# Row sums of x from a token-major copy, the layer embedding normalised in the gate, and matmuls planned with a margin

## Chip, cores and metric

One core of one Trainium2 chip. The time is device microseconds of one launch.

## What is computed

One layer of a hybrid encoder on x (2048 tokens x 1024, float32), with p (2048 x 256) as a per-layer embedding:

```
hn = RMSNorm(h) ; [u|q|k|v] = hn @ W_in
y  = concat[pool_mixer(u), per-head RMSNorm(stick_breaking_attention(q,k,v))]
h  = h + RMSNorm(y @ W_out)
h  = h + RMSNorm(sqrelu(RMSNorm(h) @ W_up) @ W_down)
h  = h + sigmoid(h @ W_gate) * RMSNorm(p @ W_ple)
```

The pooling mixer takes trailing means over 2, 4, 8 and 16 positions; the attention is strictly causal with 8 heads of 64. Every RMSNorm has a gain per channel.

## The kernel before

Tokens are cut into four chunks of 512; everything stands channel-major, a tile being 128 channels x 512 tokens, a page two of them. Each product of two float32 operands is made of three matmuls on float32r halves: every operand is split by ScalarE (the rounded half, `hi`) and VectorE (the rest, `lo`); `mm3` and `proj` issue the triples. Names in the trace: `pl` the bank of p @ W_ple, `e` its tiles, `dn` a bank of a projection, `dw` a bank of W_down, `nm` a bank of a norm, `z`, `tp`, `op` banks of attention, `act` a normalised and split input, `xp` a page of x, `qk` split q, k and pooled tiles, `wh`/`wl` split weights, `acc` the W_down sums.

A norm's factor per token is a sum over channels, that is over partitions. `add_square` squares tile after tile (ScalarE) and adds the squares into `nrm` (VectorE, or POOL where it is passed); `norm` sums the columns of `nrm` with four one-column matmuls against ones (`nm<-ones,nrm`), `rstd` turns the 128 x 4 sums into factors (`ms` on VectorE, a power on POOL, `rs` on VectorE), and `spread` brings them back to all partitions: a transpose (`nm<-ident,rs`), a masked copy on VectorE (`rt`) and a matmul (`nm<-rt,sel`). `row_rstd` copies that to a page.

`prenorm` loads x of a chunk in four pages, squares and adds its eight tiles, and multiplies each by its gain and the factor (`xp<-xp,gains,nrm`) before the split. `ple` makes the embedding of a chunk: eight `pl` banks, evicted to `e`, squared, added by POOL, then normalised by VectorE (`e<-e,gains,nrm`) and stored to HBM in four pages. `gate` loads those pages much later; per tile it takes the sigmoid (ScalarE), multiplies by the embedding and adds to h (VectorE), and stores the result. `build` starts with `ple` of all four chunks, `prenorm` of chunks 0 and 1 between them, then the input projections; attention of one chunk runs among the projections and the feed-forward of others.

The order of the instructions is not that of the code. Every operation is recorded by class `Plan` with a priority, which is the TensorE work recorded before it (the constants at the top, T_PRE, T_PLE, T_ATT, R_ATT and so on, place the parts against each other). `deadlines` carries due times back from the consumers; `order` then runs a model of the engines with a price table (`cost`), hand-over times (`LATENCY`), 53 pages, 28 small tiles and 8 PSUM banks, and on each engine takes the ready operation that is due first. What it picks becomes the fixed order of each engine's instructions; on the chip each engine then waits by semaphores only. An operation's readiness in the model is one line:

```
o.ready = max(o.ready, pick.end + LATENCY[e][o.engine])
```

A bank or page that comes free is counted apart from that. All transfers are issued from SP's queue, in order.

Of the kernel before, what the change touches and what calls it, by code (L numbers as in the profile page):

```python
# [21 lines left out]
P = 128  # L22
S = 2048
D = 1024
# [17 lines left out]
PAGES = 53  # L42
BANKS = ("pl", "dn", "nm", "z", "tp", "op", "dw")
SMALL = ("ms", "rs", "halo")
T_PRE = (11.649, 22.588)
T_PLE = (0.0, 24.403, 53.992, 45.124)
T_IN = 52.377
T_ATT = 148.286
R_ATT = 4.515
R_MAIN = 1.159  # L50
T_END = 0.0
G_IN = 4
G_GATE = 3
G_OUT = 11
NORM_LAG = (34.149, 9.928)


class Buf:
# [78 lines left out]
class Engine:  # L137
# [8 lines left out]

CROSS = {"pe": 0.2, "act": 0.15, "dve": 0.155, "pool": 0.16, "sp": 0.1}
BUSY = {"pe": 0.0, "act": 2.1, "dve": 3.9, "pool": 3.4, "sp": 1.1}
LATENCY = {
    "pe": {"pe": 0.003, "act": 0.2, "dve": 0.2, "pool": 0.2, "sp": 0.1},  # L150
    "act": {"pe": 0.27, "act": 0.142, "dve": 0.13, "pool": 0.17, "sp": 0.1},
# [4 lines left out]


SLACK = 8.348
EVICT = -0.454
AHEAD = {'pe': 40.856, 'act': 24.695, 'dve': 39.763, 'pool': 35.657, 'sp': 42.237}  # L160
LEAD = {'pe': 3.156, 'act': 0.736, 'dve': 0.004, 'pool': 1.033, 'sp': 1.169}
TAIL = 40.0
WINDOW = 4096 / 1200.0

# [28 lines left out]
class Plan:  # L193
# [165 lines left out]
    def order(self):  # L359
# [42 lines left out]
        while len(result) < len(ops):  # L402
            if not events:
                raise RuntimeError(f"order: stuck after {len(result)} of {len(ops)}")
            now = heapq.heappop(events)
            while events and events[0] <= now:
                heapq.heappop(events)
            while frees and frees[0][0] <= now:
                used[heapq.heappop(frees)[2].kind] -= 1
            moved = True  # L410
            while moved:
                moved = False
                for e in CROSS:
                    p = pending[e]
                    while p and p[0][0] <= now:
                        _, prio, seq = heapq.heappop(p)
                        heapq.heappush(waiting[e], (prio, seq))
                    if free[e] > now or not waiting[e]:
                        continue
                    skipped = []  # L420
                    pick = None
                    limit = line[front].prio + AHEAD[e]
                    while waiting[e] and waiting[e][0][0] <= limit:
                        item = heapq.heappop(waiting[e])
                        if can(ops[item[1]]):
                            pick = ops[item[1]]
                            break
                        skipped.append(item)
                    for item in skipped:
                        heapq.heappush(waiting[e], item)  # L430
                    if pick is None:
                        continue
                    moved = True
                    for b in pick.allocs:
                        b.placed = True
                        used[b.kind] += 1
                        if b.first > front:
                            live[b.kind][front:b.first] += 1
                    if e == "sp":
                        free[e] = now + pick.dur[0] + 0.03  # L440
                        dma = max(dma, now + pick.dur[0] + 0.65) + pick.dur[1]
                        pick.end = dma + 0.85
                    elif e == "pe":
                        pick.end = free[e] = clock.run(now, pick.dur)
                    else:
                        pick.end = free[e] = now + pick.dur
                    heapq.heappush(events, free[e])
                    result.append(pick)
                    gone[pick.place] = True
                    while gone[front]:  # L450
                        front += 1
                    front = min(front, len(ops) - 1)
                    for b in pick.bufs:
                        b.users -= 1
                        b.end = max(b.end, pick.end + CROSS[e])
                        if not b.users and b.real is None:
                            heapq.heappush(frees, (b.end, id(b), b))
                            heapq.heappush(events, b.end)
                    for o in after[pick.seq]:
                        o.left -= 1  # L460
                        o.ready = max(o.ready, pick.end + LATENCY[e][o.engine])
                        if not o.left:
                            heapq.heappush(pending[o.engine], (o.ready, o.prio, o.seq))
                            heapq.heappush(events, o.ready)
# [15 lines left out]
class Net:  # L480
# [152 lines left out]
            self.sp.dma_start(out=t, in_=dram[:, 2 * k2:2 * k2 + 2, :])  # L633
        return t

    def prenorm(self, dram, which):
        ts = [self.load2(dram, k2, "xp") for k2 in range(4)]
        nrm = None
        for k in range(NK):
            nrm = self.add_square(nrm, ts[k // 2][:, k % 2, :])  # L640
        r = self.row_rstd(nrm)
        acts = []
        for k in range(NK):
            t = ts[k // 2][:, k % 2, :]
            self.dve.scalar_tensor_tensor(out=t, in0=t, scalar=self.g(which, k), in1=r, op0=ALU.mult, op1=ALU.mult)
            acts.append(self.pair("act", t))
        return acts
# [230 lines left out]
    def ple(self, c, p_in, dd):  # L878
        t = self.page("pin")
        with self.plan.early(12.0):  # L880
            self.sp.dma_start(out=t, in_=p_in[c])
        acts = [self.pair("pp", t[:, k, :]) for k in range(2)]
        es = []
        nrm = None
        for ot in range(NK):
            ps = self.bank("pl")
            cs = slice(ot * P, (ot + 1) * P)
            self.mm3(ps, [(self.ple_w[k][0][:, cs], self.ple_w[k][1][:, cs], acts[k][:, 0, :], acts[k][:, 1, :])
                          for k in range(2)])
            if ot % 2 == 0:  # L890
                es.append(self.page("e"))
            m = es[-1][:, ot % 2, :]
            self.act.copy(m, ps)
            nrm = self.add_square(nrm, m, self.pool)
        r = self.row_rstd(nrm)
        for k in range(NK):
            m = es[k // 2][:, k % 2, :]
            self.dve.scalar_tensor_tensor(out=m, in0=m, scalar=self.g(G_PLE, k), in1=r, op0=ALU.mult, op1=ALU.mult)
            if k % 2:
                self.sp.dma_start(out=dd["e"][c][:, k - 1:k + 1, :], in_=es[k // 2])  # L900


    def mlp_ups(self, gi, acts, w_up, dd, first, tag):
# [49 lines left out]
        return acts  # L953

    def gate(self, cs, acts, w_gate, dd, out, first):
        for ot in range(NK):
            j = ot % 2
            if j == 0:
                ge, gh, gs = [[self.page(t) for _ in cs] for t in ("geh", "geh", "gs")]
                for i, c in enumerate(cs):  # L960
                    self.sp.dma_start(out=ge[i], in_=dd["e"][c][:, ot:ot + 2, :])
                    self.sp.dma_start(out=gh[i], in_=dd["h2"][c][:, ot:ot + 2, :])
            unit = self.weight(w_gate[ot], dd["w_gate"][ot], first)
            for i, c in enumerate(cs):
                ps = self.bank("dn")
                self.proj(ps, unit, acts[i])
                s, h = gs[i][:, j, :], gh[i][:, j, :]
                self.act.activation(s, ps, AF.Sigmoid)
                self.dve.tensor_tensor(out=s, in0=s, in1=ge[i][:, j, :], op=ALU.mult)
                self.dve.tensor_tensor(out=h, in0=h, in1=s, op=ALU.add)  # L970
                if c == NCH - 1:
                    self.sp.dma_start(out=out[c][:, ot, :], in_=h)
                elif j:
                    self.sp.dma_start(out=out[c][:, ot - 1:ot + 1, :], in_=gh[i])


def build(tc, x, p, gains, w_in, w_v, w_pool, w_out, w_up, w_down, w_gate, w_ple, out):
    with (
        tc.tile_pool(name="dram", bufs=1, space=DRAM) as dp,
        tc.tile_pool(name="const", bufs=1) as cp,  # L980
# [8 lines left out]
        def dram(name, shape):  # L989
            return plan.fixed(dp.tile(shape, F32, name="d_" + name), shape)  # L990

        dd = {n: [] for n in ("q", "k", "v", "y", "h1", "h2", "e")}
        for c in range(NCH):
            dd["q"].append([dram(f"q{c}{j}", [2, HD, 2, CH]) for j in range(NPAIR)])
            dd["k"].append([dram(f"k{c}{j}", [2, 2, HD, CH]) for j in range(NPAIR)])
# [1 line left out]
            dd["y"].append([dram(f"y{c}{k}", [P, 2, CH]) for k in range(NK)])  # L997
            for n in ("h1", "h2", "e"):
                dd[n].append(dram(f"{n}{c}", [P, NK, CH]))
        for n, m in (("w_in", 12), ("w_v", 4), ("w_out", NK), ("w_up", NF), ("w_down", NF), ("w_gate", NK)):  # L1000
            dd[n] = [[dram(f"{n}{i}{a}", [P, D]) for a in range(2)] for i in range(m)]

# [3 lines left out]
        acts = {}  # L1006
        for c in range(2):
            plan.at(T_PRE[c])
            acts[c] = net.prenorm(x[c], G_PRE)
            plan.at(T_PLE[c + 1])  # L1010
            net.ple(c + 1, p, dd)
        plan.at(T_PLE[3])
# [1 line left out]

        def project(c):
            if c > 1:
                acts[c] = net.prenorm(x[c], G_PRE)
            net.in_proj(c, w_in, w_v, acts[c], dd)
            net.u_proj(c, w_in, acts[c], dd)

# [104 lines left out]
```

## Time and profile before

| | us |
|---|---|
| median of 3 runs (2662.93 to 2663.47) | 2663.43 |
| the profiled execution, its own time | 2662.55 |
| its span, first to last instruction | 2660.8 |
| TensorE busy (share) | 2626.7 (99%) |
| weight loads busy | 2146.5 (81%) |
| VectorE, ScalarE, POOL busy | 1709.8 (64%), 1037.3 (39%), 726.6 (27%) |

668 MB pass the DMA engines. Every operation stands under one line, L275, the helper that issues a recorded call, so the rows are told apart by tile names. Weight loads overlap matmuls. A TensorE that is busy 99% can still be slow, since a matmul counts as busy while it goes through; the granted clock has to be read beside it.

### The profile page before, as it was taken

The page shows a single profiled execution, that of the slowest core. Times are in us where ns is not written, and L with a number is a line of the kernel's source. Part 1 is how long each engine was busy: PE and PEld are TensorE (multiplying, and loading weights), DVE is VectorE, ACT ScalarE, POOL GpSimd, SP SyncE. Part 2 cuts the span into 40 slices and gives each one's busy share as a digit, 9 for nine tenths or more (in the row PEclk, how much of TensorE's full clock was granted, in tenths as well). Part 3 has the DMA queues.
Part 4 walks back from the last instruction along what each step waited for, and adds up shares of the span by engine and source line. Part 5 has one row for each costly group of instructions (what it writes and reads, how often), then busy time and mean ns, then how long its engine had stood idle before and what let it go on. Part 6 is the DMA issues. An engine that isn't in the chain of part 4 may idle for free.

```text
span 2660.8 us, 34134 instructions
## 1 busy us (share of the span) xinstructions
PE 2626.7 (99%) x12312; PEld 2146.5 (81%) x12312; DVE 1709.8 (64%) x2331; ACT 1037.3 (39%) x1907; POOL 726.6 (27%) x663
## 2 busy tenths in 40 slices
PE   8999999999999999999999999999999999999999
PEld 6778787777888888888888888888887888888887
DVE  7854748868777759967665568685667273433454
ACT  8433536446445445445333343443334122111111
POOL 5432335344233323323333223333334000000000
PEclk9899999999999999999999999999999999999999
DMA  6899878878777758747955476475754675555576
GB/s 260 318 370 348 287 261 327 277 242 331 258 258 257 293 190 335 280 157 279 355 192 190 159 260 252 163 257 201 281 202 158 258 270 196 207 193 196 201 287 239
DMA packets 213129, 668.41 MB, mean 251 GB/s; under 512 B 22880, under 2 KB 39264, under 8 KB 212960
## 3 DMA queue, kind: packets, MB, share of 16 engines
q1 hardware_dynamic: 212960, 666.22, 69.8%
q8 instruction: 98, 1.61, 0.2%
q14 instruction: 71, 0.58, 0.1%
HBM read 489.97 MB, written 176.16 MB: 250 GB/s over the span
## 4 chain that ended last, share of the span: by engine, by line
PE 91%; DVE 4%; DMA 1%; ACT 1%; issue 1%; POOL 1%; SPq 0%; ACTq 0%; DVEq 0%; POOLq 0%
PE dn L275 50%; PE dw L275 26%; PE op L275 4%; PE z L275 4%; PE tp L275 4%; PE nm L275 2%; DVE q L275 1%; POOL nrm L275 1%; ACT nrm L275 1%; DMA wl<-d_w_up 0%; DMA d_y<-ypool 0%; DVE nrm L275 0%; DVE e L275 0%; DVE at L275 0%; POOL pt L275 0%
## 5 line engine op out<-in xcount | busy, mean ns | idle before, releaser
L275 PE MATMUL dn<-act,wh 128*128 128x512 f32 x2816 | 901.4, 401 | 4.3 <-ACT act L275 2.2
L275 POOL TENSOR_TENSOR pr<-pr,q 128x1 f32<-128x1 f32 (+4 forms) x512 | 564.5, 1115 | 1116.0 <-ACT pr L275 481.6
L275 PE MATMUL dw<-m,wh 128*128 128x512 f32 x2048 | 644.7, 396 | 3.0 <-DVE acc L275 3.0
L275 PEld LDWEIGHTS dn<-act,wh 128*128 128x128 f32 x2816 | 510.8, 190 | 103.0 <-issue 5.3
L275 PE MATMUL dn<-act,wl 128*128 128x512 f32 x1408 | 553.0, 393 | 0.0
L275 DVE TENSOR_TENSOR_SCAN q<-q,ones 128x512 f32<-128x512 f32 (+1 forms) x320 | 401.7, 1268 | 95.2 <-ACT q L275 94.0
L275 PEld LDWEIGHTS dw<-m,wh 128*128 128x128 f32 x2048 | 374.1, 188 | 76.3 <-DVE acc L275 3.4
L275 DVE TENSOR_TENSOR acc<-acc,dw 128x512 f32<-128x512 f32 x480 | 324.8, 681 | 139.1 <-PE dw L275 137.5
L275 PE MATMUL dw<-m,wl 128*128 128x512 f32 x1024 | 400.0, 391 | 0.0
L275 PEld LDWEIGHTS dn<-act,wl 128*128 128x128 f32 x1408 | 265.9, 189 | 57.8
L275 ACT CAST at<-tp 128x512 fp32r<-128x512 f32 (+1 forms) x320 | 166.5, 524 | 302.5 <-PE tp L275 271.9
L275 DVE TENSOR_TENSOR at<-tp,at 128x512 fp32r<-128x512 f32 (+1 forms) x320 | 191.1, 602 | 125.6 <-ACT at L275 125.2
L275 DVE TENSOR_TENSOR rl<-rl 128x512 f32<-128x512 f32 x128 | 97.7, 764 | 263.7 <-ACT rl L275 263.4
L275 ACT ACTIVATE q<-z 128x512 f32<-128x512 f32 (+1 forms) x320 | 171.3, 537 | 239.0 <-PE z L275 227.7
L275 ACT ACTIVATE rl<-dn 128x512 f32<-128x512 f32 x128 | 76.6, 598 | 472.3 <-PE dn L275 462.6
L275 PEld LDWEIGHTS dw<-m,wl 128*128 128x128 f32 x1024 | 192.2, 188 | 41.5
L275 POOL TENSOR_TENSOR ms<-ms,mhalf 128x4 f32<-128x4 f32 (+1 forms) x36 | 55.2, 1534 | 614.8 <-DVE ms L275 614.7
L275 PE MATMUL op<-at,kv 128*128 128x512 f32 (+3 forms) x640 | 182.9, 365 | 2.0 <-DVE at L275 2.0
L275 PE MATMUL z<-kv,qd 128*128 128x512 f32 (+3 forms) x640 | 178.1, 361 | 0.0
L275 ACT ACTIVATE pr<-z 128x512 f32<-128x512 f32 (+1 forms) x320 | 170.2, 534 | 5.2 <-PE op L275 2.6
L275 PE MATMUL tp<-ident,pr 128*128 128x128 f32 x1088 | 169.7, 272 | 1.2 <-DVE acc L275 0.6
L275 PEld LDWEIGHTS tp<-ident,pr 128*128 128x128 f32 x1088 | 136.0, 140 | 39.8 <-DVE acc L275 1.1
(118 smaller groups left out, 2961.7 us busy)
## 6 DMA issues: line engine op xcount, KB each, us to landing
wh<-d_w_up SPq DMA_DIRECT2D x96, 512.0 KB, 4.9
wl<-d_w_up SPq DMA_DIRECT2D x96, 512.0 KB, 6.0
wh<-d_w_down SPq DMA_DIRECT2D x96, 512.0 KB, 5.5
wl<-d_w_down SPq DMA_DIRECT2D x96, 512.0 KB, 5.2
xin<-d_h SPq DMA_DIRECT2D x48, 512.0 KB, 7.2
kv<-d_k SPq DMA_DIRECT2D x80, 256.0 KB, 6.1
kv<-d_v SPq DMA_DIRECT2D x80, 256.0 KB, 6.6
wh<-d_w_in SPq DMA_DIRECT2D x36, 512.0 KB, 8.1
```

The lines of the kernel that those rows point to most:

```text
L275: fn(*[a.real() if isinstance(a, Ref) else a for a in args], **{k: a.real() if isinstance(a, Ref) else a for k, a in kw.items()})
```

## The change

It does three things, and sets new values for the planner's constants.

1. x is passed a second time, token-major (`xr`, 128 tokens x 1024). `prenorm` loads four such tiles per chunk, and ScalarE squares each with a running sum over its row, which gives the sums per token directly: no squares of x tiles, no adds, no matmuls against ones. `rstd` and `spread` follow as before.
2. `ple` stores `e` unnormalised, page by page as it is evicted, and adds the squares on VectorE; the factor row goes to HBM as a tile of its own (`er`). `gate` loads that row, multiplies by embedding and gain in one instruction, by the row in a second, and adds.
3. In the planner an operation of TensorE is ready 2 us later than its input from another engine.

```diff
+MARGIN = 2.0
...
-T_ATT = 148.286
-R_ATT = 4.515
+T_ATT = 158.048
+R_ATT = 4.132
...
-                        o.ready = max(o.ready, pick.end + LATENCY[e][o.engine])
+                        late = MARGIN if o.engine == "pe" and e != "pe" else 0.0
+                        o.ready = max(o.ready, pick.end + LATENCY[e][o.engine] + late)
...
+    def token_sums(self, rows):
+        sums = self.plan.tile([P, 16], F32, "ms")
+        for b in range(4):
+            t = self.plan.tile([P, D], F32, "xr")
+            with self.plan.early(8.0):
+                self.sp.dma_start(out=t, in_=rows[b])
+            self.act.activation(t, t, AF.Square, accum_out=sums[:, b:b + 1])
+        return sums[:, 0:4]
-    def prenorm(self, dram, which):
+    def prenorm(self, dram, rows, which):
+        rs = self.rstd(self.token_sums(rows), 4, D)
         ts = [self.load2(dram, k2, "xp") for k2 in range(4)]
-        nrm = None
-        for k in range(NK):
-            nrm = self.add_square(nrm, ts[k // 2][:, k % 2, :])
-        r = self.row_rstd(nrm)
+        with self.plan.resumed(self.plan.t + NORM_LAG[1]):
+            bank = self.spread(rs, self.bank("nm"))
+        r = self.page("nrm")[:, 1, :]
+        self.act.copy(r, bank)
...
-            nrm = self.add_square(nrm, m, self.pool)
-        r = self.row_rstd(nrm)
-        for k in range(NK):
-            m = es[k // 2][:, k % 2, :]
-            self.dve.scalar_tensor_tensor(out=m, in0=m, scalar=self.g(G_PLE, k), in1=r, op0=ALU.mult, op1=ALU.mult)
-            if k % 2:
-                self.sp.dma_start(out=dd["e"][c][:, k - 1:k + 1, :], in_=es[k // 2])
+            nrm = self.add_square(nrm, m)
+            if ot % 2:
+                self.sp.dma_start(out=dd["e"][c][:, ot - 1:ot + 1, :], in_=es[-1])
+        self.sp.dma_start(out=dd["er"][c], in_=self.row_rstd(nrm))
...
+        rows = []
+        for c in cs:
+            rows.append(self.page("er")[:, 0, :])
+            self.sp.dma_start(out=rows[-1], in_=dd["er"][c])
...
-                self.dve.tensor_tensor(out=s, in0=s, in1=ge[i][:, j, :], op=ALU.mult)
+                self.dve.scalar_tensor_tensor(out=s, in0=s, scalar=self.g(G_PLE, ot), in1=ge[i][:, j, :], op0=ALU.mult,
+                                              op1=ALU.mult)
+                self.dve.tensor_tensor(out=s, in0=s, in1=rows[i], op=ALU.mult)
                 self.dve.tensor_tensor(out=h, in0=h, in1=s, op=ALU.add)
```

The new constants (T_PRE, T_PLE, G_IN, NORM_LAG, EVICT, AHEAD, LEAD beside the two above) and the margin change the order on every engine. Three places:

VectorE while chunk 0 is projected, around a norm's masked copy `rt`. Before:

```order
47 L275 TENSOR_TENSOR wl<-ws,wh 128x1024
48 L275 SCALAR_TENSOR_TENSOR e<-e,gains,nrm 128x512
49 L275 CAST rs<-ms 128x4
50 L275 SCALAR_TENSOR_TENSOR e<-e,gains,nrm 128x512
51 L275 TENSOR_TENSOR qk<-dn,qk 128x512
52 L275 TENSOR_TENSOR rs<-ms,rs 128x4
53 L275 SCALAR_TENSOR_TENSOR e<-e,gains,nrm 128x512 x6
54 L275 TENSOR_TENSOR rt<-nm,pick_84 8x512
55 L275 TENSOR_TENSOR qk<-dn,qk 128x512
56 L275 TENSOR_TENSOR wl<-ws,wh 128x1024 x3
```

With the change:

```order
64 L276 TENSOR_TENSOR nrm<-nrm 128x512 x3
65 L276 TENSOR_TENSOR qk<-dn,qk 128x512
66 L276 TENSOR_SCALAR ms<-nm 128x4
67 L276 TENSOR_TENSOR nrm<-nrm 128x512
68 L276 CAST rs<-ms 128x4
69 L276 TENSOR_TENSOR wl<-ws,wh 128x1024
70 L276 TENSOR_TENSOR rs<-ms,rs 128x4
71 L276 TENSOR_TENSOR nrm<-nrm 128x512
72 L276 TENSOR_TENSOR qk<-dn,qk 128x512
73 L276 TENSOR_TENSOR rt<-nm,pick_84 8x512
74 L276 TENSOR_TENSOR nrm<-nrm 128x512
75 L276 TENSOR_TENSOR wl<-ws,wh 128x1024
```

The normalisations of `e` are gone, and the adds of squares (`nrm`) stand in ones and twos between the splits.

TensorE at the start, the embedding's matmuls and the first two norms. Before:

```order
3 L275 MATMUL pl<-pp,plew 128x512 x6
4 L275 MATMUL nm<-ones_76,nrm 128x1 x4
5 L275 MATMUL pl<-pp,plew 128x512 x9
6 L275 MATMUL nm<-ident,rs 8x128
7 L275 MATMUL pl<-pp,plew 128x512 x6
8 L275 MATMUL nm<-rt,sel_92 128x512
9 L275 MATMUL pl<-pp,plew 128x512 x6
10 L275 MATMUL nm<-ident,rs 8x128
```

With the change:

```order
1 L276 MATMUL pl<-pp,plew 128x512 x48
2 L276 MATMUL nm<-ident,rs 8x128
3 L276 MATMUL pl<-pp,plew 128x512 x15
4 L276 MATMUL nm<-rt,sel_92 128x512
5 L276 MATMUL pl<-pp,plew 128x512 x27
6 L276 MATMUL nm<-ident,rs 8x128
7 L276 MATMUL pl<-pp,plew 128x512 x18
8 L276 MATMUL nm<-rt,sel_92 128x512
9 L276 MATMUL pl<-pp,plew 128x512 x15
```

The column sums ahead of the first transpose are gone, the transpose comes after 48 matmuls, and 15 and 18 matmuls stand between it and the spread.

SP's queue at the start. Before:

```order
2 L275 DMA pin<-in_p 128x1024
3 L275 DMA ws<-in_w_ple 128x512 x4
4 L275 DMA xp<-in_x 128x1024 x2
5 L275 DMA pin<-in_p 128x1024
6 L275 DMA xp<-in_x 128x1024 x3
7 L275 DMA pin<-in_p 128x1024
8 L275 DMA xp<-in_x 128x1024 x2
9 L275 DMA ws<-in_w_in 128x1024
10 L275 DMA pin<-in_p 128x1024
11 L275 DMA xp<-in_x 128x1024
12 L275 DMA ws<-in_w_in 128x1024 x5
13 L275 DMA ws<-in_w_v 128x1024 x2
```

With the change:

```order
2 L276 DMA pin<-in_p 128x1024
3 L276 DMA ws<-in_w_ple 128x512 x4
4 L276 DMA xr<-in_xr 128x1024 x4
5 L276 DMA pin<-in_p 128x1024
6 L276 DMA xr<-in_xr 128x1024 x4
7 L276 DMA pin<-in_p 128x1024
8 L276 DMA ws<-in_w_in 128x1024
9 L276 DMA xp<-in_x 128x1024 x2
10 L276 DMA pin<-in_p 128x1024
11 L276 DMA xp<-in_x 128x1024
12 L276 DMA d_e_156<-e 128x1024
13 L276 DMA xp<-in_x 128x1024
```

Eight row copies go ahead of x and of the first weights, and stores of `e` stand among the loads.

## Rows read from the trace of the kernel before

**Rows 1.** The page: span, engines' busy us, one group (count, busy us, mean ns).
```profile
span 2660.8 us, 34134 instructions
...
PE 2626.7 (99%) x12312; PEld 2146.5 (81%) x12312; DVE 1709.8 (64%) x2331; ACT 1037.3 (39%) x1907; POOL 726.6 (27%) x663
...
L275 DVE TENSOR_TENSOR rl<-rl 128x512 f32<-128x512 f32 x128 | 97.7, 764 | 263.7 <-ACT rl L275 263.4
```

**Rows 2.** TensorE's waits, who ended them: us in total, times, longest.
```profile
PE pl L275 <- ACT plew L275: 6.9, 1, 6.9
PE nm L275 <- DVE rt L275: 5.9, 2, 3.6
PE dw L275 <- DVE acc L275: 3.0, 1, 3.0
PE nm L275 <- DVE rs L275: 2.2, 2, 2.0
PE dn L275 <- DVE at L275: 2.2, 1, 2.2
PE dn L275 <- ACT act L275: 2.2, 1, 2.2
PE dn L275 <- DVE act L275: 2.1, 3, 1.7
PE op L275 <- DVE at L275: 2.0, 6, 0.5
...
PE dn L275 <- DVE qk L275: 0.3, 1, 0.3
```

**Rows 3.** The chain of waits at the end: start, us, what.
```profile
2592.91 62.80 PE dn L275 x276
...
2657.09 0.69 DVE geh L275
```

**Rows 4.** By stretch: PE, PEld, DVE, ACT, POOL us; PEclk, DMA share, GB/s.
```profile
40.00:70.00 30.00, 29.61 (x132) 23.32 (x131) 28.73 (x34) 22.92 (x41) 21.24 (x11) 1.00 0.49 181
70.00:104.00 34.00, 28.11 (x98) 21.81 (x98) 28.79 (x36) 16.03 (x27) 20.53 (x13) 0.80 0.81 301
104.00:270.00 166.00, 165.65 (x786) 134.37 (x785) 93.29 (x143) 64.55 (x124) 41.12 (x38) 1.00 1.02 357
270.00:300.00 30.00, 26.04 (x123) 20.17 (x122) 27.97 (x45) 20.10 (x44) 15.98 (x13) 0.89 0.57 193
...
400.00:460.00 60.00, 56.97 (x271) 46.41 (x270) 54.72 (x61) 42.13 (x78) 37.35 (x28) 0.97 0.87 317
```

**Rows 5.** The timeline of VectorE, 55 to 78 us: start, us, what.
```profile
64.50 10.30 DVE L275 SCALAR_TENSOR_TENSOR e<-e,gains,nrm 128x512 f32<-128x512 f32 x6
74.73 0.67 DVE L275 TENSOR_TENSOR rt<-nm,pick 8x512 fp32r<-8x512 f32 x1
```

**Rows 6.** Groups of VectorE's instructions, 2050 to 2661 us.
```profile
L275 DVE TENSOR_TENSOR rl<-rl 128x512 f32<-128x512 f32 x42 | 29.0, 692 | 161.5 <-ACT rl L275 161.5
...
L275 DVE SCALAR_TENSOR_TENSOR acc<-acc,gains,nrm 128x512 f32<-128x512 f32 x16 | 11.0, 749 | 2.1 <-ACT nrm L275 2.1
```

**Rows 7.** Groups of all engines' instructions, 0 to 100 us.
```profile
L275 POOL TENSOR_TENSOR nrm<-nrm 128x512 f32<-128x512 f32 x28 | 51.9, 1870 | 37.2 <-ACT nrm L275 37.2
...
L275 DVE SCALAR_TENSOR_TENSOR e<-e,gains,nrm 128x512 f32<-128x512 f32 x9 | 14.7, 1675 | 0.6 <-ACT nrm L275 0.6
...
L275 DVE TENSOR_TENSOR nrm<-nrm 128x512 f32<-128x512 f32 x14 | 12.5, 893 | 9.2 <-ACT nrm L275 9.1
```

**Rows 8.** Groups of TensorE's instructions by shape, whole span.
```profile
L275 PE MATMUL nm<-ones,nrm 128*128 128x1 f32 x160 | 19.9, 245 | 0.6 <-POOL nrm L275 0.5
```

**Rows 9.** The chain of waits at the start: start, us, what.
```profile
3.60 6.42 DMA xp<-in_x
```

**Rows 10.** Two more stretches, columns as in rows 4.
```profile
10.00:20.00 10.00, 10.00 (x45) 8.22 (x44) 4.99 (x6) 8.72 (x17) 2.60 (x2) 1.00 1.03 415
2200.00:2400.00 200.00, 200.00 (x886) 165.19 (x886) 80.05 (x122) 32.25 (x53) 1.40 (x1) 1.00 0.54 194
```

More of the change, by code (lines that the diff above doesn't have):

```diff
@@ L44 @@
 SMALL = ("ms", "rs", "halo")
-T_PRE = (11.649, 22.588)
-T_PLE = (0.0, 24.403, 53.992, 45.124)
+T_PRE = (12.427, 26.975)
+T_PLE = (0.0, 23.664, 53.992, 38.428)
 T_IN = 52.377
-T_ATT = 148.286
-R_ATT = 4.515
+T_ATT = 158.048
+R_ATT = 4.132
 R_MAIN = 1.159
 T_END = 0.0
-G_IN = 4
+G_IN = 6
 G_GATE = 3
 G_OUT = 11
-NORM_LAG = (34.149, 9.928)
+NORM_LAG = (33.412, 9.928)
 class Buf:
@@ L158 @@
 SLACK = 8.348
-EVICT = -0.454
-AHEAD = {'pe': 40.856, 'act': 24.695, 'dve': 39.763, 'pool': 35.657, 'sp': 42.237}
-LEAD = {'pe': 3.156, 'act': 0.736, 'dve': 0.004, 'pool': 1.033, 'sp': 1.169}
+EVICT = -0.605
+AHEAD = {'pe': 42.752, 'act': 24.695, 'dve': 39.763, 'pool': 24.241, 'sp': 42.237}
+LEAD = {'pe': 3.156, 'act': 0.736, 'dve': 0.004, 'pool': 1.033, 'sp': 1.078}
 TAIL = 40.0
@@ L974, in gate, with build @@
                     self.sp.dma_start(out=out[c][:, ot - 1:ot + 1, :], in_=gh[i])
-def build(tc, x, p, gains, w_in, w_v, w_pool, w_out, w_up, w_down, w_gate, w_ple, out):
+def build(tc, x, xr, p, gains, w_in, w_v, w_pool, w_out, w_up, w_down, w_gate, w_ple, out):
     with (
@@ L990, in dram @@
             return plan.fixed(dp.tile(shape, F32, name="d_" + name), shape)
-        dd = {n: [] for n in ("q", "k", "v", "y", "h1", "h2", "e")}
+        dd = {n: [] for n in ("q", "k", "v", "y", "h1", "h2", "e", "er")}
         for c in range(NCH):
@@ L999, in build @@
                 dd[n].append(dram(f"{n}{c}", [P, NK, CH]))
+            dd["er"].append(dram(f"er{c}", [P, CH]))
         for n, m in (("w_in", 12), ("w_v", 4), ("w_out", NK), ("w_up", NF), ("w_down", NF), ("w_gate", NK)):
@@ L1008, in build @@
             plan.at(T_PRE[c])
-            acts[c] = net.prenorm(x[c], G_PRE)
+            acts[c] = net.prenorm(x[c], xr[c], G_PRE)
             plan.at(T_PLE[c + 1])
@@ L1016, in project @@
             if c > 1:
-                acts[c] = net.prenorm(x[c], G_PRE)
+                acts[c] = net.prenorm(x[c], xr[c], G_PRE)
             net.in_proj(c, w_in, w_v, acts[c], dd)
@@ L1102 @@
         "x": _chunks(np.asarray(x)[0]),
+        "xr": np.asarray(x)[0].reshape(NCH, CH, D)[:, ::-1].reshape(NCH, 4, P, D),
         "p": _chunks(np.asarray(p)[0, 0]),
```

## The prediction

> **What bounds the kernel now.** I read the page's engine shares first: TensorE is busy 2626.7 of 2660.8 us [rows 1], so only what holds TensorE up matters. The list of TensorE's waits came next [rows 2]: the first row is the start, and the other eleven sum to 21.6 us. The rest of the idle time is the end, 5.1 us from the last matmul at 2655.71 [rows 3] to the span's end. Then the table by stretch, for the granted clock [rows 4]. Where its mean is under 1.00, TensorE ran part of the stretch at the lower of its two levels, 1.2 instead of 2.4 GHz, and the time lost is length times (1 - clock): 34 x 0.20 = 6.8 us in 70 to 104, 30 x 0.11 = 3.3 us in 270 to 300, 60 x 0.03 = 1.8 us in 400 to 460, together 11.9 us. Before each of these TensorE waited, so it goes when the wait goes. Waits and clock, 33.5 us, are what an order that never lets TensorE wait could win.
>
> By name the waits are of four kinds [rows 2]. **`rt`**: 5.9 us in two pieces, both in 70 to 104. VectorE shows why [rows 5]: the small `rt` stood behind six `e` normalisations, 10.30 us in a row, 1.7 us each. Alone such an instruction takes 0.75 us (the `acc` row [rows 6], same operation and shape); beside them POOL was adding squares, 28 adds of 1870 ns, with VectorE's own adds at 893 [rows 7]. **`act`**: 2.2 + 2.1 us, where the first matmuls of chunk 2 come before their operand; the low clock in 270 to 300 goes with it. **Inputs that come a little late**: `rs` 2.2, `at` 2.2 and 2.0, and three small ones, 7.8 us, spread over the span. **`acc`**: 3.0 us and a small one, 3.6, an add that has to free a PSUM bank. (Three rows under 0.7 us are left out ahead of the last; with it they are 2.0.)
>
> **The change, part by part.**
>
> *Early VectorE queue.* The 32 `e` normalisations leave this stretch, as do 14 adds of prenorm's squares (9 and 14 fall within the first 100 us: 14.7 + 12.5 = 27.2 us [rows 7]); the 28 adds of POOL come to VectorE, 28 x 0.69 (a product of that shape in a POOL-free stretch [rows 6]) = 19.3 us. POOL is left with the `ms` powers, so the slowing beside it should go as well. The order bears it out: ahead of the `rt` now stand single adds and `qk` or `wl` splits, no row of six. I take 11.7 of the 5.9 + 6.8 = 12.7 us; ends 0 and 12.7. Next late there would be a `wl` split.
>
> *Chunk 2.* Its chain loses seven adds of squares and a set of column sums, but the order shows TensorE as short of work as before: between chunk 2's `nm<-rt` and its first `dn<-act` stand 4.2 us of matmuls instead of 1.4 us, while that chain needs a copy, four normalisations at 0.75, a cast and a subtraction, and two `o` steps stand between: eight or nine steps of about 0.7 us, some 6 us. A wait of 2 us remains, with some low clock. I take 3 of 4.3 + 3.3 = 7.6 us; ends 0 and 7.6.
>
> *The margin.* The planner now calls a matmul ready 2 us later than its input from another engine. The first spread of a norm, for one, has 15 matmuls between its two halves where it had 6. Counted over both whole orders at 0.227 us per 512 columns (62.80 us for 276 of them [rows 3]), waits of TensorE with under 2.5 us of matmuls between the last matmul they depend on and themselves were 43 and are 20; 14 stand in the chunk-2 hole in either order, so elsewhere 29 become 6. From the third kind, with its clock, 7.8 + 1.8 = 9.6 us, I take 7.5; ends 0 and 9.6. The margin acts on inputs, not on a bank coming free, so of the 3.6 us for `acc` I take 1.5.
>
> *Small terms.* Sixteen column-sum matmuls of prenorm go: 19.9 / 160 = 0.124 us each [rows 8], 2.0 us. The end grows: behind the last sigmoid stood a product and a sum, 0.7 us each [rows 3]; now one instruction of 0.75 and two of 0.69, +0.75 us. ScalarE changes 32 squares for 16 twice as long, which is no more work. The eight er transfers (256 KB each) and the gate's extra multiplies are covered: VectorE is busy 64% [rows 1].
>
> *The start.* The eight row copies of chunks 0 and 1 come ahead of x on SP, and four squares ahead of the first `e<-pl` on ScalarE. The first x copy lands at 3.60 + 6.42 = 10.0 us [rows 9]; a row copy takes its place, and three more follow at 0.52 MB / 415 GB/s = 1.26 us [rows 10], the last at 13.8. One square more, about 1.1 us, and the first eviction starts near 15 us. Eight PSUM banks of six matmuls last from 6.9 to 17.8 us: covered. The second p tile is two transfers later (2.5 us), which may show: +1 us; ends 0 and +4.
>
> *New waits.* A wholly new order has new misses; I put +4, ends 0 and 21.6 (as many as now).
>
> A rule that speaks against the gate's part: the Trainium skill (SBUF — State Buffer, "Who interferes with whom") says that a VectorE instruction with two SBUF inputs and a GpSimd instruction that reads SBUF lock each other out for a whole instruction. By it each of the 16 added multiplies of the first two gates could stand behind a whole POOL instruction, and nothing would be won at `acc`. What the rows show there is milder: the `rl` product takes 764 ns over the whole span [rows 1], 692 where POOL is idle [rows 6]. By the rule the result would be 2645 or 2646.
>
> **Sum.** -11.7 - 3 - 7.5 - 1.5 - 2.0 + 0.75 + 1 + 4 = -20 us against the profiled execution's own 2662.55 (span 2660.8 and 1.75 around it): 2642.6. The median shown, 2663.43, lies 0.9 higher, so 2643.5. With every term at its good end: -12.7 - 7.6 - 9.6 - 3.6 - 2.0 + 0.75 = -34.8, 2629.
>
> The Trainium skill (Perfetto Trace Analysis, "Identifying the Most-Contended Engine") holds matmul busy time for a bad measure and weight-load busy for a good one. Taken against the gapless stretch 2200 to 2400, where weight loads fill 165.2 / 200 = 82.6% [rows 10], the 2146.5 us of them [rows 1] would need 2599 us: 62 us of room instead of 33.5. No wait is named for the other 28, so they are not in the range.
>
> **Rivals.** *The waits only move.* The planner's prices are not the chip's (an `e` step of 0.75 us took 1.7), so a new order can miss as often as the old. Then the new waits are 21.6 and not 4, and the result is 2643.5 + 17.6 = 2661. That the margin does nothing on the chip ends here too. The count of 43 to 20 speaks against it. Chance 0.11.
>
> *The transfers become the bound.* Until 270 us the kernel moves 12 row copies of 0.52 MB and four er rows, 7.3 MB more. Between 104 and 270 the DMA engines are at 1.02 of their time and move 357 GB/s [rows 4]: there 7.3 MB cost 20.5 us. Between 40 and 104 us there is idle DMA time of 30 x 0.51 + 34 x 0.19 = 22 us, so it just fits, and only if SP's in-order queue fills it. SP stood there because its stores wait for their data, and the order now puts `e` stores, which wait for ScalarE, between the weight loads. If hardly any of it is filled, weights come late by 20.5 us, and the clock falls behind the waits; at the cheapest ratio seen (1.8 us of clock for the 2.2 us wait and two small ones, 3.0, in 400 to 460) that is 33 us: 2676. It decides once some 15 of the 20.5 us are not absorbed. Against it: TensorE has no wait on a transfer today but the start, and the store of each `e` tile no longer waits for its norm. Chance 0.12, slower.
>
> **How the numbers follow.** The forecast has 0.72, the rivals 0.11 and 0.12, the rest lies between. The forecast's own range is 2629 to 2656. To leave out no more than 2 in 10 I go up to 2664: the first rival in, most of the second out. 0.2% is 5.3 us, about what a measurement of this kernel can tell from no change. Faster: the forecast, part of the first rival and of the rest, 0.75; within: 0.11; slower: 0.14.
>
> **What would show it.** Early queue: no wait of TensorE on `rt` over 1 us before 110 us and clock 1.00 between 40 and 104; `e` gone from VectorE's products there, its `nrm` adds near 0.69 us. Margin: TensorE's waits past 300 us under 6 us in sum, clock 1.00 in 400 to 460. Chunk 2: a wait for `act` near 270 us remains. End: three VectorE instructions behind the last sigmoid. Wrong: waits on landings of `wl` or `xp` between 30 and 270 us, or as many waits on VectorE as now in new places.

## The result

The changed kernel takes **2639.29 us** (median of 4 runs, 2638.64 to 2640.74) where the kernel before, timed beside it, takes 2663.18 (2660.91 to 2663.47): a ratio of 0.9913, 95% interval 0.9896 to 0.993. That is 23.9 us less, against the 20 forecast, and 4.2 us under the predicted 2643.5. The profiled execution took 2640.74 us, 21.8 less than the 2662.55 of the one before. Its page:

```profile
span 2638.9 us, 34111 instructions
...
PE 2612.6 (99%) x12280; PEld 2135.4 (81%) x12280; DVE 1702.4 (65%) x2331; ACT 1030.8 (39%) x1907; POOL 680.8 (26%) x635
```

The busy times of VectorE and POOL fell by 7 and 46 us [rows 1], neither of which sets the end. TensorE's waits, which answer to [rows 2] (us in total, times, longest):

```profile
PE pl L276 <- ACT plew L276: 7.2, 1, 7.2
PE op L276 <- DVE at L276: 6.2, 4, 1.8
PE nm L276 <- DVE rt L276: 1.8, 2, 0.9
PE op L276 <- issue: 1.4, 1, 1.4
PE dn L276 <- DVE act L276: 0.9, 2, 0.7
PE dw L276 <- DVE at L276: 0.9, 1, 0.9
PE tp L276 <- DVE acc L276: 0.7, 1, 0.7
PE dn L276 <- ACT act L276: 0.6, 1, 0.6
PE nm L276 <- DVE rs L276: 0.4, 1, 0.4
PE dn L276 <- DVE qk L276: 0.3, 1, 0.3
```

Here `plew` is the split W_ple and `pp` the split p, `pr` a page of attention weights, `at` its transposed and split copy, `o` the attention output. Besides the start the waits are 13.2 us, 21.6 before. `rt` went from 5.9 to 1.8, `acc` (3.0) is gone, but `op<-at` grew from 2.0 to 6.2. The stretches, in the columns of [rows 4] (PE, PEld, DVE, ACT, POOL busy us with counts; granted clock, DMA share, GB/s), first of the changed kernel:

```profile
0.00:40.00 40.00, 31.93 (x132) 24.72 (x132) 22.36 (x47) 34.01 (x64) 4.46 (x45) 1.00 0.95 371
40.00:70.00 30.00, 30.00 (x135) 24.34 (x135) 26.27 (x39) 27.66 (x50) 1.99 (x1) 1.00 1.03 418
70.00:104.00 34.00, 34.00 (x156) 27.24 (x155) 15.09 (x22) 13.17 (x18) 3.55 (x5) 1.00 0.98 364
104.00:270.00 166.00, 163.97 (x793) 133.59 (x791) 89.38 (x140) 69.70 (x147) 52.89 (x48) 1.00 1.02 351
270.00:300.00 30.00, 27.53 (x136) 21.35 (x137) 29.64 (x46) 16.02 (x35) 14.85 (x10) 1.00 0.73 249
300.00:400.00 100.00, 98.44 (x481) 79.25 (x480) 60.65 (x79) 42.31 (x85) 38.29 (x34) 1.00 0.81 281
400.00:460.00 60.00, 59.95 (x294) 48.55 (x293) 42.69 (x57) 38.62 (x75) 24.45 (x20) 1.00 1.03 404
460.00:590.00 130.00, 128.19 (x619) 103.05 (x618) 102.99 (x143) 64.37 (x128) 61.31 (x47) 0.99 0.73 250
590.00:1800.00 1210.00, 1205.56 (x5800) 986.86 (x5800) 906.86 (x1160) 553.08 (x1014) 418.18 (x376) 1.00 0.69 246
1800.00:2060.00 260.00, 260.00 (x1213) 214.13 (x1212) 141.62 (x194) 69.26 (x128) 56.10 (x48) 1.00 0.63 233
2060.00:2661.00 601.00, 573.06 (x2538) 472.37 (x2536) 264.84 (x412) 102.58 (x171) 4.78 (x4) 1.00 0.59 217
```

The same cuts of the kernel before, as far as [rows 4] don't show them:

```profile
0.00:40.00 40.00, 32.39 (x141) 25.81 (x142) 23.93 (x40) 32.63 (x60) 17.60 (x55) 1.00 0.85 323
...
300.00:400.00 100.00, 99.77 (x492) 80.59 (x491) 52.97 (x82) 34.96 (x73) 30.05 (x29) 1.00 0.84 294
...
460.00:590.00 130.00, 129.93 (x630) 105.20 (x630) 91.44 (x135) 60.06 (x118) 41.40 (x36) 1.00 0.78 266
590.00:1800.00 1210.00, 1206.89 (x5787) 988.01 (x5786) 879.38 (x1146) 544.63 (x993) 403.59 (x357) 1.00 0.69 248
1800.00:2060.00 260.00, 255.69 (x1229) 210.00 (x1228) 164.66 (x203) 94.63 (x179) 91.31 (x81) 1.00 0.59 212
2060.00:2661.00 601.00, 595.70 (x2640) 490.82 (x2638) 263.95 (x412) 104.66 (x176) 6.43 (x5) 1.00 0.62 228
```

From these, idle time plus length times (1 - clock), before and after, gives a ledger of TensorE's lost time:

| stretch | before | after | difference |
|---|---|---|---|
| 0 to 104 us | 13.9 + 6.8 clock | 8.1 | -12.6 |
| 104 to 300 | 4.3 + 3.3 clock | 4.5 | -3.1 |
| 300 to 1800 | 6.4 + 1.8 clock | 7.9 + 1.3 clock | +1.0 |
| 1800 to 2060 | 4.3 | 0 | -4.3 |
| 2060 to the span's end | 5.1 | 5.8 | +0.7 |

That is -18.3 of the span's -21.9 us. The other 3.6 go with work that is gone: TensorE has 32 matmuls fewer (12312 and 12280), all of them column sums (x160 in [rows 8], now x128):

```profile
L276 PE MATMUL nm<-ones,nrm 128*128 128x1 f32 x128 | 15.1, 239 | 0.0
```

### The profile page after: what moved, and what is told of

Same layout as the page of the kernel before. It is cut to its first block, busy times and chain, and to the rows that moved or that the text cites. A ratio compares the mean times of both kernels' runs of the same rounds, so it can differ in the third digit from the quotient of the medians.

```text
span 2638.9 us, 34111 instructions
## 1 busy us (share of the span) xinstructions
PE 2612.6 (99%) x12280; PEld 2135.4 (81%) x12280; DVE 1702.4 (65%) x2331; ACT 1030.8 (39%) x1907; POOL 680.8 (26%) x635
## 4 chain that ended last, share of the span: by engine, by line
PE 92%; DVE 5%; DMA 1%; ACT 1%; issue 1%; POOL 0%; SPq 0%; DVEq 0%; ACTq 0%
PE dn L276 50%; PE dw L276 26%; PE z L276 5%; PE op L276 4%; PE tp L276 4%; PE nm L276 2%; DVE q L276 1%; PE pl L276 1%; DMA wl<-d_w_in 1%; DVE at L276 0%; DVE wl L276 0%; DVE ypool L276 0%; DMA xr<-in_xr 0%; DVE act L276 0%; DVE qk L276 0%
## 5 line engine op out<-in xcount | busy, mean ns | idle before, releaser
L276 DVE TENSOR_TENSOR_SCAN q<-q,ones 128x512 f32<-128x512 f32 (+1 forms) x320 | 409.3, 1293 | 87.0 <-ACT q L276 85.4
```

Of the source, the lines that this page charges most:

```text
L276: fn(*[a.real() if isinstance(a, Ref) else a for a in args], **{k: a.real() if isinstance(a, Ref) else a for k, a in kw.items()})
```

## The experiments

The theory was that the terms are separate and add up: 13 us of the start by taking the normalisations and POOL's adds out of one another's way, 7 or so by the margin, the rest small. The main rival was the prediction's own first one, that the waits only move with each new order. Every kernel is one edit of the kernel before or of the changed one; its time is told with its ratio to the kernel before, timed beside it, and the 95% interval of that ratio.

**1. The changed kernel without the margin.**

```diff
-MARGIN = 2.0
+MARGIN = 0.0
```

> The changed kernel with the margin set to 0, all else as in it. Theory (early VectorE queue worth about 12 us, margin about 8): no wait on rt over 1 us before 110 us and clock 1.00 there, but small waits on rs, rt and at come back after 110 us; 2645 to 2650 us. Rival (the margin does it all): the early waits come back too, 2655 to 2663.

Measured: 2654.46 us, ratio 0.9969 (0.9958 to 0.998). Up to 104 us it is as good as with the margin, and the waits stand later:

```profile
PE op L276 <- DVE at L276: 8.5, 6, 2.1
...
PE tp L276 <- POOL pr L276: 5.5, 5, 3.1
```

The `pr` waits are new; 4.9 us of them stand at 1054 to 1060 us, and in 1060 to 1080 the granted clock is 0.88. So the early gain doesn't need the margin. In this program the margin is worth 15 us, which lies between the two expectations: the theory gave it 8, the rival the whole gain.

**2. The kernel before with the margin alone.** The edit is the change's two lines in the planner.

```diff
+MARGIN = 2.0
-                        o.ready = max(o.ready, pick.end + LATENCY[e][o.engine])
+                        late = MARGIN if o.engine == "pe" and e != "pe" else 0.0
+                        o.ready = max(o.ready, pick.end + LATENCY[e][o.engine] + late)
```

> The kernel before with the 2 us margin alone. Theory: the waits past 300 us shrink by 5 to 8 us, but the wait on rt behind the e normalisations at 70 to 104 us and its low clock stay; 2652 to 2658 us. Rival (the margin does it all): 2640 to 2645.

Measured: 2664.99 us, ratio 1.0003 (0.9993 to 1.0013): no difference, and both expectations missed. The rows of 70 to 104 and of 270 to 300 us:

```profile
70.00:104.00 34.00, 29.36 (x110) 22.95 (x110) 29.16 (x36) 17.07 (x29) 15.12 (x11) 0.85 0.86 323
...
270.00:300.00 30.00, 25.50 (x115) 19.17 (x114) 28.81 (x44) 18.65 (x42) 19.11 (x15) 0.73 0.67 226
```

The early fall of the clock stays (0.85), and 270 to 300 got worse: 0.73, 8.1 us, where it was 0.89 [rows 4]. A margin that is worth 15 us in one program is worth nothing in the other.

**3. The kernel before, every engine's order as it was, POOL's adds cut short.** POOL still does the 28 adds of squares, at the same places, but on one of 512 columns; so the row sums of the layer embedding are left out.

```diff
-            nrm = self.add_square(nrm, m, self.pool)
+            nrm = self.add_square(nrm, m, self.pool, 1)
```

> The kernel before, every instruction in the same order, but POOL's 28 adds of the embedding's squares work on 1 of 512 columns (left out: the sum of the squares of the embedding in the other 511 columns). Theory (POOL and VectorE hold each other up, so that rt comes late): the six e steps take 0.75 us each instead of 1.7, the waits on rt in 70 to 104 go, with the clock there; 2649 to 2653 us, waits past 110 us as before. Rival (the queue order alone makes rt late): e steps stay at 1.7 us or the wait stays over 2 us; 2660 to 2664.

Measured: 2649.85 us, ratio 0.9952 (0.9937 to 0.9967), 13 us less with no instruction moved. VectorE's timeline at the place of [rows 5]:

```profile
58.41 4.06 DVE L281 SCALAR_TENSOR_TENSOR e<-e,gains,nrm 128x512 f32<-128x512 f32 x6
65.93 0.68 DVE L281 TENSOR_TENSOR rt<-nm,pick 8x512 fp32r<-8x512 f32 x1 [3.46 <-PE nm L281]
```

The six `e` steps take 4.06 us in place of 10.30, and now it is `rt` that waits, for TensorE. POOL's own queue is shorter too, a second way for `rt` to come earlier, but a small one: from the start of the `ms` step ahead of this row to the row's end VectorE took 18.9 us before and 7.7 here, and of that it stood idle for a result of POOL for 0.9 and 0.2 us. The rest is longer steps. In 70 to 104 us TensorE is busy throughout at full clock:

```profile
70.00:104.00 34.00, 34.00 (x156) 27.38 (x155) 28.14 (x44) 20.61 (x32) 6.46 (x12) 1.00 0.98 361
```

Its later waits are those of before (`acc` 3.0, `rs` 2.2, `at` 2.2, `act` 2.2). This is the cleanest of the runs: the early term is shown, with its cause (POOL's adds) and its size, and the row of six `e` steps is still there.

**4. The changed kernel with the planner constants of before** (`T_PRE` to `LEAD` as in the diff's minus lines; margin and code of the change kept).

```diff
-G_IN = 6
+G_IN = 4
...
-EVICT = -0.605
+EVICT = -0.454
...
```

> The changed kernel with the planner's constants (start times, rates, AHEAD, LEAD, EVICT, NORM_LAG, G_IN) of the kernel before, margin kept. Theory (the constants are fine tuning): 2639 to 2647 us. Rival (the constants carry the gain): over 2652.

Measured: 2650.32 us, ratio 0.9953 (0.9938 to 0.9968), between the two. The late wait on a bank is back, and with it the place of 400 to 460 us:

```profile
400.00:460.00 60.00, 57.33 (x267) 46.99 (x268) 40.83 (x52) 36.14 (x70) 23.76 (x22) 0.94 0.97 356
...
1800.00:2060.00 260.00, 257.00 (x1232) 211.86 (x1231) 176.40 (x222) 93.52 (x177) 93.42 (x82) 0.99 0.60 212
```

TensorE's wait in the second stretch is the one of the kernel before [rows 2]:

```profile
PE dw L276 <- DVE acc L276: 3.0, 1, 3.0
```

Every kernel run here with the new constants is busy for 260.00 of the 260 us of 1800 to 2060, with or without the margin and the code parts; every one with the old constants waits there. So the `acc` term, 3 to 4 us, belongs to the constants; which of them does it was not tried. In all the constants are worth 11 us in the changed program (2650.32 against 2639.29), nearly half of its gain, and the prediction gave them no price.

**5. The changed kernel with the old row sums of x.**

```diff
-        rs = self.rstd(self.token_sums(rows), 4, D)
...
+        nrm = None
+        for k in range(NK):
+            nrm = self.add_square(nrm, ts[k // 2][:, k % 2, :])
+        r = self.row_rstd(nrm)
```

> The changed kernel with x's row sums taken as before, by VectorE adds and 4 column-sum matmuls per chunk; layer embedding, gate, margin and planner constants as in the change. Theory that the parts add up: the 16 column-sum matmuls come back (+2 us) and VectorE has about 12 us more in the first 100 us, now without GpSimd beside it: 2640 to 2646 us, 70 to 104 us at a granted clock of 0.97 or more. Rival, that the order and its constants fit only the whole: 2650 to 2657 us, with new waits on VectorE and ScalarE after 250 us, as with the old constants.

Measured: 2649.63 us, ratio 0.995 (0.9935 to 0.9964), just below the rival's range and above the theory's. (The 16 column sums of the text are 32 in the trace.) Up to 104 us nothing is lost, though VectorE has some 20 us more to do there; the time goes at one place:

```profile
270.00:300.00 30.00, 25.93 (x95) 18.82 (x96) 28.45 (x43) 14.79 (x28) 15.49 (x10) 0.72 0.59 200
```

30 x 0.28 = 8.4 us of clock, behind a wait of 2.5 us on `rs` at 271. With the 32 matmuls (3.6 to 4.0 us) that is more than the whole 10.3.

**6. The changed kernel with the old layer embedding**: POOL's adds and the normalisation back in its stage, the gate as before. **9. The changed kernel with only the 28 adds back on POOL**, which leaves the normalisation in the gate and nearly the same order on TensorE.

```diff
-            nrm = self.add_square(nrm, m)
+            nrm = self.add_square(nrm, m, self.pool)
```

> The changed kernel with the layer embedding squared and summed on GpSimd and normalised in its own stage as before; x's row sums from the token-major copy, margin and constants as in the change. Theory that GpSimd's adds stretch VectorE's steps at the start: the wait on the weights of rt or a like one comes back between 60 and 90 us with the clock fall behind it, 2647 to 2654 us. Rival, that the lighter VectorE (no adds for x) and the margin cover the contention: 2639 to 2645 us, 70 to 104 us at a granted clock over 0.97, though the e steps stay at 1.4 us or more.

> The changed kernel with the 28 adds of the layer embedding's row sums back on GpSimd; its normalisation stays in the gate stage, TensorE's order is the same but for a few places in the first 100 us. Theory A, that the e steps in VectorE's early queue were what GpSimd's adds made harmful: the adds run to GpSimd's end beside other VectorE work, VectorE's queue is short, and the time stays at 2638 to 2643 us with 70 to 104 us at a granted clock of 0.97 or more. Theory B, that any VectorE step beside GpSimd's adds is stretched enough: a wait on rt, rs, pp or act of 2 us or more comes back in the first 100 us, 2645 to 2652 us.

Measured: 2648.88 us, ratio 0.9947 (0.9932 to 0.9962), for 6 and 2647.14 us, 0.9945 (0.993 to 0.996), for 9: the theory in 6, theory B in 9. The waits of 9, 10 to 110 us, and what VectorE did then:

```profile
PE pl L276 <- DVE pp L276: 4.2, 2, 3.4
```

```profile
32.16 4.13 DVE L276 SCALAR_TENSOR_TENSOR xp<-xp,gains,nrm 128x512 f32<-128x512 f32 x3
36.21 1.75 DVE L276 TENSOR_TENSOR pp<-pin,pp 128x512 fp32r<-128x512 f32 x1
37.88 1.76 DVE L276 SCALAR_TENSOR_TENSOR xp<-xp,gains,nrm 128x512 f32<-128x512 f32 x1
```

The `e` steps aren't there, and yet 0 to 104 us lose 6.8 us to the changed kernel (11.3 of idle time and 3.5 of clock, against 8.1): now the `xp` steps take 1.4 to 1.8 us and `pp` 1.75, which is 0.69 without POOL beside it. So the `e` queue is not needed for the loss; POOL's adds beside other VectorE work that TensorE waits for are enough. Moving the normalisation into the gate and leaving the adds on POOL keeps about half of this term. Between 6 and 9, which differ by the normalisation's move alone, lie 1.7 us. The adds' move without the normalisation's was not run, so that it carries the larger part is likely, but not shown.

**7. The kernel before with the margin and all new constants**, and none of the moved work.

> The kernel before with the margin and all of the change's planner constants, but none of its two moves of work. Theory that the parts add up: the changed kernel's 2639.3, plus 13 us of the start and 2 us of matmuls: 2651 to 2656 us. Rival, that margin and constants gain only in the changed program: 2660 to 2667 us, as with the margin alone.

Measured: 2656.83 us, ratio 0.9977 (0.9967 to 0.9986), 17.5 us over the changed kernel where the sum gave 15, or 17 with the column sums counted rightly; that is 0.8 us above the theory's range and 3 below the rival's. It loses at the start and at 270 us:

```profile
70.00:104.00 34.00, 30.27 (x125) 23.83 (x124) 31.28 (x42) 20.23 (x33) 19.22 (x14) 0.90 0.91 336
...
270.00:300.00 30.00, 22.95 (x101) 15.89 (x100) 29.45 (x49) 19.81 (x44) 18.78 (x13) 0.83 0.45 155
```

**8, 10, 11. The changed kernel with margins of 3, 1.75 and 2.25 us.**

```diff
-MARGIN = 2.0
+MARGIN = 3.0
```

> The changed kernel with a margin of 3 us in place of 2. Theory that the margin covers lateness and the rest is set by TensorE's own work: the 4 waits on VectorE's attention product (6.2 us) shrink, 2636 to 2641 us. Rival, that each order has waits of its own and 2 us fits the constants it came with: 2645 to 2656 us with waits at other places of 300 to 1100 us.

> The changed kernel with a margin of 1.75 us. Theory that a margin of that size does the work whatever the order: 2637 to 2643 us. Rival, that part of the changed kernel's time is the particular order that 2 us and these constants give, above all a stretch of 265 to 300 us in which the clock does not fall: 2645 to 2656 us, with half clock there.

> The changed kernel with a margin of 2.25 us. Theory that a margin of that size does the work whatever the order: 2637 to 2643 us. Rival, that part of the changed kernel's time is the particular order that 2 us and these constants give: 2645 to 2656 us, as with 3 us (2655), with half clock at 265 to 300 us or a wait over 3 us behind it.

Measured: with 3 us 2655.34, ratio 0.9973 (0.9962 to 0.9983); with 1.75 us 2641.84, 0.9928 (0.9911 to 0.9944); with 2.25 us 2648.44, 0.9951 (0.9936 to 0.9966). There is no trend: at 1.75 us the theory holds, at 2.25 and 3 the rival. What tells 2 from 2.25 is one place, first with 1.75, then with 2.25:

```profile
270.00:300.00 30.00, 27.23 (x124) 21.97 (x125) 29.29 (x45) 16.20 (x36) 16.17 (x10) 0.89 0.68 224
...
270.00:300.00 30.00, 24.09 (x88) 17.76 (x89) 25.98 (x40) 14.11 (x27) 12.51 (x8) 0.72 0.66 233
```

In the changed kernel this row is 27.53 at 1.00, and with 3 us 24.18 at 0.72. TensorE's timeline around it, with the idle time ahead of each piece in brackets, at 2.25 us:

```profile
271.69 0.50 PE L276 MATMUL nm<-rt,sel 16*128 16x512 f32 x1 [2.03 <-DVE rt L276]
...
276.62 1.87 PE L276 MATMUL nm<-half,o 128*128 128x2 f32 x8 [1.73 <-DVE o L276]
```

with the clock at 0.83 between the two and 0.50 behind:

```profile
270.00:275.00 5.00, 3.19 (x15) 2.17 (x15) 5.00 (x5) 1.16 (x3) 5.00 (x3) 0.83 0.93 321
```

and at 2 us:

```profile
270.24 0.50 PE L276 MATMUL nm<-rt,sel 16*128 16x512 f32 x1 [0.88 <-DVE rt L276]
...
273.59 0.47 PE L276 MATMUL dn<-act,wh 128*128 128x512 f32 x1 [0.64 <-ACT act L276]
...
274.74 0.50 PE L276 MATMUL dn<-act,wh 128*128 128x512 f32 x1 [0.68 <-DVE act L276]
```

Chunk 2 is short of matmuls in both. Behind the wait of 2.03 us the clock went to the lower level, before the wait of 1.73 began, and stayed there to 290 us; behind 0.88 and a few of some 0.6 it did not fall. With 1.75 us of margin there are waits of 0.88, 1.36 and 1.24 us, and the row at 0.89 shows 3.3 us of clock: the fall does not need a wait of 2 us.

**12. The changed kernel with the margin behind VectorE's results alone.**

```diff
-                        late = MARGIN if o.engine == "pe" and e != "pe" else 0.0
+                        late = MARGIN if o.engine == "pe" and e == "dve" else 0.0
```

> The changed kernel with the margin of 2 us only behind VectorE's results, none behind those of ScalarE, GpSimd and the transfers. Theory that it is VectorE that runs later than planned (its wait groups hold most of TensorE's waiting): 2637 to 2645 us, no wait group of ScalarE over 2 us. Rival, that the others need it as well: 2648 to 2656 us, with new waits on GpSimd's pr or ScalarE's pr, act or plew.

Measured: 2641.78 us, ratio 0.9925 (0.991 to 0.994), as the theory said; no wait on ScalarE but the start. Against experiment 1 the margin behind VectorE alone brings 12.7 of the 15 us; what it adds behind the others is too small to tell here. None of the twelve beats the changed kernel; 10 and 12 are within 0.2% of it.

## Why the prediction was right, and where it was not

Direction and size came out, but the terms did not all hold; their misses nearly cancelled, which is luck.

- **Early VectorE queue and start** (-11.7 and +1, -10.7): -12.6. All 12.7 us went; a new wait on `rt` of 0.9 us at 35 us came in, and the start cost 0.3 (7.2 for 6.9). The sign set for it held: no wait on `rt` over 1 us, clock 1.00 from 40 to 104 us. The size is confirmed at fixed order (13 us in experiment 3). Of the reason the slowing beside POOL is right, and the row of six `e` steps is not needed for it: experiment 3 keeps the row and loses nothing, and experiment 9 loses without it.
- **Chunk 2** (-3): -3.1 for 104 to 300 us. The wait forecast is there, split into small ones, but without the low clock. That the size was met is in part luck: in experiments 5, 8 and 11 the clock falls there for 8.4 us, in 10 for 3.3.
- **Margin and new waits** (-7.5 and +4, -3.5): +1.0 for 300 to 1800 us. This step failed. The count of tight matmuls (43 to 20, taken from the orders; no row shows it) points the same way as the margin's good in experiment 1, but it priced lateness as if the waits left would be the old ones. In the old order `dn<-at` waited 2.2 us in 400 to 460; in the new one that wait is gone, and `op<-at` waits four times between 300 and 630, 6.2 us in sum. The first rival, that waits only move, is what happened in this stretch. Of the two signs set for the margin, clock 1.00 in 400 to 460 came, and waits past 300 us under 6 us in sum did not: they are 7.8. A margin's worth is no number of its own: 15 us in the changed program, 0 in the old one, and 9 us less for a quarter of a microsecond more.
- **`acc`** (-1.5 of 3.6): 1800 to 2060 us gave 4.3, 3.6 of it waits on `acc`. The term was mis-sized because its cause was sought in the margin; experiments 1, 4 and 7 show that it is the constants. The Trainium skill's lock rule (SBUF — State Buffer, "Who interferes with whom") would have left it at 0; since the gain came with the constants, this stretch doesn't test the rule. At the start, where POOL's adds are whole-tile and VectorE's `pp` took 1.75 us for 0.69 (experiment 9), the trace agrees with it. The prediction called the rows milder than the rule from a mean, 764 ns for 692, and a mean over products of which only some stand beside work of POOL cannot say that. Singly (least, median, most, in ns, in the kernel before) the longest takes 2.7 times the median:

```profile
L275 DVE TENSOR_TENSOR rl<-rl x128: 659/692/1841, 614.1 to 2547.5; 128x512 f32<-128x512 f32 x128
```

- **Column sums** (-2.0): -3.6 to -4.0, the first what the ledger leaves, the second counted. The edit takes out 16 in the program, and the trace has two records for each: 32 x 0.124 = 4.0. The row and the count were not in the same unit.
- **End** (+0.75): +0.7, as forecast. The three VectorE instructions are there:

```profile
2633.73 0.75 DVE L276 SCALAR_TENSOR_TENSOR gs<-gs,gains,geh 128x512 f32<-128x512 f32 x1 [0.51 <-ACT gs L276]
2634.51 0.69 DVE L276 TENSOR_TENSOR gs<-gs,er 128x512 f32<-128x512 f32 x1
2635.24 0.69 DVE L276 TENSOR_TENSOR geh<-geh,gs 128x512 f32<-128x512 f32 x1
```

- **Transfers as the bound** (the slower rival): they filled the idle time of 40 to 70 us, at 418 GB/s and a share of 1.03 where it was 0.49 [rows 4], and no wait in TensorE's list is on a transfer. The idle DMA time absorbed them.

What stays open: why one order has two long waits in chunk 2 and the next has small ones was read from the traces, not caused by an edit of its own; the constants were not tried on the kernel before without the margin, nor one by one; and the embedding's adds were not moved without its normalisation. Whether 2 us is the best margin can't be said either, since each margin here ran with constants that came with 2.

## What to carry to other kernels

When an engine off the critical path slows another, cut its work short with every order kept and read the price: 13 us here, and the one number in this study that stood by itself. A re-planned order has no price per part: forecast it as a spread (margins of 0 to 3 us gave 2639 to 2655 us here with the same work), and look for the one stretch short of matmuls where a wait of 1 to 2 us can take the clock with it. Before multiplying a row's mean, see that the count of the edit and the count of the row are of the same thing.

## What the runs showed that was not expected

- POOL's adds and VectorE's whole-tile steps slow each other. With the adds cut to one column the `e` steps took 4.06 / 6 = 0.68 us, not 1.7; in experiment 9 the `xp` steps took 1.4 to 1.8 us and `pp` 1.75. The adds took 1870 ns in the mean [rows 7]; the first one, begun while VectorE was idle, took 1.30 us:

```profile
14.69 1.30 POOL L275 TENSOR_TENSOR nrm<-nrm 128x512 f32<-128x512 f32 x1 [11.51 <-ACT nrm L275]
```

- What the clock adds can be several times the wait before it: in experiment 11 it fell behind a wait of 2.03 us and cost 8.4 us, while the changed kernel has 2.5 us of idle time in 270 to 300, in pieces under 1 us, and no fall.
- In experiment 2 a re-planned program of the same work on the same engines came out within 0.1% of the old one, with its waits at other places.
